# An attention stage's hand-written order, rewritten: new places for every step of a head, one batch in eight on TensorE, small operations on GpSimd

## The chip, the cores and the metric

One core of a Trainium2 chip runs the whole program. The metric is device time in microseconds (us) of one execution; lower is better. Five engines work side by side, each through its own queue in program order: TensorE (PE; its weight loads are listed as PEld), VectorE (DVE), ScalarE (ACT), GpSimd (POOL) and SyncE (SP), which here only issues DMA transfers. An engine stops at an instruction whose input or buffer isn't ready, and everything behind it in that queue waits too.

## The reference, cut to what matters

A two-layer decoder handles a prompt of 256 tokens and 8 sample sequences of 8 tokens together: a convolution layer, an MLP, an attention layer, an MLP. Only the attention layer is touched. It has 8 heads and three key groups per head, (window, dilation) = (128, 1), (512, 4), (2048, 16). For the samples each query sees its own tokens and cached keys at distances d, 2d, ..., window:

```python
idx = n_past + arange(S)[:, None] - dilation * arange(window // dilation + 1)[None, :]
s = einsum('bshe,bsnhe->bhsn', q, k_cat[:, idx]);  p = softmax(where(idx >= 0, s, -1e30))
o = einsum('bhsn,bsnhe->bshe', p, v_cat[:, idx])   # per group
# the three groups are merged by their softmax denominators, then  x += o @ w_o
```

Three groups merged this way are one softmax over all keys, and so the kernel computes it. At dilation 16 no two sample queries share a cached key, so there the product is elementwise: each query's vector times its own 128 keys, summed. That is done per batch (8 of them per head), once for keys and once for values.

## The kernel before, in words

Activations lie transposed, 128 channels by T = 320 tokens (256 prompt, 64 sample). Every fp32 product is three matmuls of fp32r halves: a weight is split by `split` (L117 to L127 of the kernel before) into `wh`, rounded by ScalarE (L126), and `wl`, the rest, subtracted by VectorE (L127), in halves of 1024 columns. Both have four buffers in a ring (`bufs=4`); raw weights have four of 1 MB, filled by SyncE.

In the attention stage nothing is scheduled automatically. Each step is added to a list with a position, and the list is sorted by position. Head h's weights (query, key and value for three groups: 9 chunks of 4 quarters) make 36 steps at positions 36h to 36h+35, 12 matmuls each; one position is thus one such step plus what is woven in. The rest of head h-1's attention (`side`) stands at 36h plus an offset, so it runs between the next head's 36 steps. After the last head the 32 steps of the output product `wo` take the place of the 36.

`Stream.run` walks the sorted list. Before a step that uses half number n of the weights it emits the splits up to half n+3 (`AHEAD = 3`); with four buffers the split of half n+3 has to wait until TensorE has finished with half n-1. A step's follow-up (`post`: the evacuation of its PSUM result by ScalarE or VectorE) is emitted after the next TensorE step. So one engine's queue holds splits and follow-ups mixed, and a split that waits for TensorE holds up what is behind it.

Steps of a head that matter below, with their offsets before:

- `qk` (3.2, 4.2, 5.2, 6.2 for dilation 4; 7.2 for dilation 1): sample scores of two groups, each step one half of split cached keys. Follow-up L811 to L813.
- `p_s(1)` (9.2): scores of the second 128 prompt rows, `o<-k,q` L746; its follow-up is a row maximum (L754, VectorE), exp (L618), reciprocal (L619), scaling (L620).
- `s_soft` (9.8): the same for the sample scores `S`: maximum over groups L822, then L618 to L620 on `S`.
- `p_t(1)` (13.6, 13.9): transposes of the second prompt softmax, `s<-cst,Sp` L762; `s_t`, `n_t` (14.6, 14.9): those of the sample softmax, L830 and L843.
- `pv` (18 to 26.8): sample output, L860, one half of split cached values each.
- `piece` (9 + 2.2b for keys, 26.6 + 2.2b for values, b = 0 to 7): dilation 16. SyncE fetches 512 KB into one of four buffers `al` (2.9 earlier); GpSimd copies a row `R` to all partitions (L643, the query or the probabilities) and multiplies in two halves (L645); VectorE sums (L650, 4.5 later). `row` writes `R` by small DMAs; `scores2` (6) transposes the query for it (L668).
- `q_fill` (1.2): `zz<-q` on ScalarE and a 128x64 subtraction on VectorE (L708); `new_s` (2.4): scores of the new tokens (L714), mask added by VectorE (L720); `v_t` (0, 0.3, 0.6): transposed values (L695, L696); `s_end`: adds the dilation-16 part to a head's sample output `os` (L887) and splits it.

Of the kernel before, what the change touches and what calls it, by code (L numbers as in the profile page):

```python
# [24 lines left out]
F32 = mybir.dt.float32  # L25
F32R = mybir.dt.float32r
# [12 lines left out]
G = 3  # L39
# [27 lines left out]
C_ID = 0  # L67
C_I2 = 128
C_SEL = 192
C_MN = 200  # L70
C_N = C_MN + NNEW
B_ID = 0
B_MS = 128
B_MP = B_MS + NPE
B_N = B_MP + 1152
CV_TAPS = {14: (11, 12), 15: (11, 12)}


# [1 line left out]
def decoder_step(ctx: ExitStack, tc: tile.TileContext, I, O):  # L80
# [119 lines left out]
    class Norm:  # L200
# [329 lines left out]
    with tc.tile_pool(name="attn", bufs=1) as ap:  # L530
# [8 lines left out]
        cb = ap.tile([128, B_N], BF, name="cb")  # L539
        pool.dma_start(cb, I["cb"])  # L540
        idb = cb[:, B_ID:B_ID + 128]

        B = {}

# [81 lines left out]
            todo.append((pos, len(todo), (pe_, post, chunk, part)))  # L626

        E2 = {}
        slots = [0]

        def piece(kind, h, b, at):


            n = slots[0]
            slots[0] += 1
            t = spread[:, n % 4]

            def fetch():
                sp.dma_start(t, I[kind + "2"][h, b])

            def mult():
                wide = spread[:, 4]
                pool.partition_broadcast(wide, E2[kind, h, b // 4][32 * (b % 4):32 * (b % 4) + 1, :])  # L643
                for c in (0, 512):
                    pool.tensor_mul(t[:, c:c + 512], t[:, c:c + 512], wide[:, c:c + 512])  # L645
# [7 lines left out]
            add(at - 2.9, None, fetch)  # L653
            add(at, None, mult)
            add(at + 4.5, None, total)

        def row(kind, h, half, src):

            r = E2[kind, h, half] = ap.tile([128, 1024], F32, name="R", bufs=2)
            for j in range(4):  # L660
                b = 4 * half + j
                sp.dma_start(r[32 * j:32 * j + 1, :], src[8 * b:8 * b + 8, :])

        def scores2(h, t0):

            def go():
                E2["qT", h] = ps = s_tile()
                pe.transpose(ps[:64, :128], B[h, 0, 2][:, SEQ:], ident)  # L668

            def post():  # L670
                q = ap.tile([64, 128], F32, name="qT")
                act.activation(q, E2["qT", h][:64, :128], AF.Copy)
                E2["q", h] = q
                row("k", h, 0, q)

            add(t0 + 6, go, post)
            add(t0 + 12, None, lambda: row("k", h, 1, E2["q", h]))
            for b in range(NB):
                piece("k", h, b, t0 + 9 + 2.2 * b)

        def side(h, t0):

# [21 lines left out]
            def q_fill():  # L704
                for g in range(2):
                    q = B[h, 0, g][:, SEQ:].rearrange("p (b s) -> p b s", b=NB)
                    act.activation(diag(g, 0), q, AF.Copy)
                    dve.tensor_sub(diag(g, 64), q, diag(g, 0))  # L708

            def new_s(pos):  # L710
                def go():
                    E["new"] = ps = s_tile()
                    for g in range(G):
                        pe.matmul(ps[:64, g * 64:g * 64 + 64], B[h, 0, g][:, SEQ:], B[h, 1, g][:, SEQ:], start=True,  # L714
                                  stop=True)

                def post():
                    E["S"] = S = ap.tile([64, NKEY + NNEW], F32, name="S")
                    E["m"] = small.tile([64, 8], F32, name="m")
                    dve.tensor_add(S[:, NKEY:], E["new"][:64, :NNEW], cst[:64, C_MN:C_MN + NNEW])  # L720
                    dve.tensor_reduce(E["m"][:, 0:1], S[:, NKEY:], axis=AX.X, op=OP.max)
                step(pos, go, post)

            def scores2_in(pos):
# [138 lines left out]

            def s_red():
                om = ap.tile([128, NB, 128], F32, name="Sp")
                E["orr"] = ap.tile([128, 128], F32, name="orr")
# [24 lines left out]
            for g in range(G):  # L891
                v_t(.3 * g, g)
            step(1.2, None, q_fill)
            new_s(2.4)
            scores2_in(2.7)
            p_s(3, 0)
            qk(0, 3.2, 4.2)
            qk(1, 5.2, 6.2)
            p_t(6.4, 0, 0)
            qk(2, 7.2)  # L900
            p_o(8.6, 0)
            p_s(9.2, 1)
            step(9.8, None, s_soft)
            p_t(13.6, 1, 0)
            p_t(13.9, 1, 3)
            s_t(14.6, 0, 5)
            n_t(14.9)
            p_o(17, 1)
            t2, dt = (13.5, 2.1) if last else (26.6, 2.2)
            step(11.5 if last else 22, None, lambda: row("v", h, 0, E["S"][:, NPE:NKEY]))  # L910
            step(11.5 if last else 30, None, lambda: row("v", h, 1, E["S"][:, NPE:NKEY]))
            for b in range(NB):
                piece("v", h, b, t0 + t2 + dt * b)
            for t in range(5):
                pv(18 + 2.2 * t, t)
            step(28.3, None, s_red)
            s_out(33.2)
            if not last:
                step(48.5, None, s_end)

        def qkv_steps(h):
            L = []
# [99 lines left out]
def _masks():  # L1022
    import numpy as np
    import ml_dtypes
    cst = np.zeros((128, C_N), np.float32)
    cst[:, C_ID:C_ID + 128] = np.eye(128)
    cst[:, C_I2:C_I2 + 64] = np.concatenate([np.eye(64), np.eye(64)])
    for p in range(128):
        cst[p, C_SEL + p % 64 // 8] = 1.0
    mn = np.full((64, G, 64), NEG, np.float32)  # L1030
    ms = np.full((128, NPE), NEG, np.float32)
    ms[64:] = 0
    mp = np.full((2, 128, G, 256), NEG, np.float32)
    for b in range(NB):
        for s in range(NS):
            p = 8 * b + s
            for g in range(G):
                for s2 in range(s + 1):
                    if (s - s2) % DILATIONS[g] == 0:
                        mn[p, g, 8 * b + s2] = 0  # L1040
            ms[p, [r for r in range(512) if r % 4 == s % 4 and r >= s]] = 0
            ms[p, [512 + r for r in range(128) if r >= s]] = 0
    for q in range(256):
        for g in range(G):
            for k in range(q + 1):
                if (q - k) % DILATIONS[g] == 0 and q - k <= WINDOWS[g]:
                    mp[q // 128, q % 128, g, k] = 0
    cst[:64, C_MN:] = mn.reshape(64, NNEW)
# [4 lines left out]
    cb[:, B_MP + 384:] = mp[1].reshape(128, 768)  # L1053
    return cst, cb.astype(ml_dtypes.bfloat16)


# [80 lines left out]
```

## Time and profile before

| | us |
|---|---|
| three runs | 3083.86, 3087.28, 3088.25 |
| median | 3087.28 |
| profiled execution, whole | 3087.17 |
| its span, first to last instruction | 3085.4 |
| TensorE busy in it | 2953.4 (96%) |
| VectorE, ScalarE, GpSimd busy | 1900.2, 1339.9, 895.9 |

The attention stage is the stretch in which GpSimd is busy a second time, from about 1365 to 2145 us. In the page's forty slices TensorE shows nine or more tenths everywhere except at the beginning and in slices 19 to 22 and 27, all in or just behind that stage. The page's chain of waits says what ended last; the view of waits says who waited for whom; timelines give the queue of one engine instruction by instruction.

### The profile page before, as it was taken

To read this page: it belongs to the slowest core of one execution; us is meant where nothing else is said; L and a number is where in the kernel's file an instruction comes from. 1 tells how busy PE (TensorE), PEld (TensorE's weight loads), DVE (VectorE), ACT (ScalarE), POOL (GpSimd) and SP (SyncE) were. 2 spreads that over 40 slices of the span, in tenths; PEclk is the share of its full clock that TensorE was granted. 3 is DMA by queue.
4 is the path that set the end of the run, shared out by engine and by line. 5 is a ranking of instruction groups with operands and counts; after the bars stand their busy time and mean duration, and the time that the engine had idled before them with its cause. 6 is when DMAs were issued, how large, how long until landed. Compare 5 with 4: busy or idle time off the path is not lost.

```text
span 3085.4 us, 47707 instructions
## 1 busy us (share of the span) xinstructions
PE 2953.4 (96%) x19600; PEld 2896.6 (94%) x19608; DVE 1900.2 (62%) x2258; ACT 1339.9 (43%) x1889; POOL 895.9 (29%) x597
## 2 busy tenths in 40 slices
PE   6999799999999999999999999988999999999998
PEld 6998799999999999999888888987999999999998
DVE  7989755444444444566898888888644444444444
ACT  7878544334334334434444444444433433433442
POOL 2767200000000000025999998996100000000000
PEclk9999899999999999999999999998999999999999
DMA  5443244444444444456767767765444444444442
GB/s 191 139 139 134 96 150 147 149 149 150 148 149 149 150 151 150 151 183 224 281 244 269 266 236 274 282 225 198 162 149 149 149 149 149 150 150 150 149 151 89
DMA packets 96522, 533.64 MB, mean 173 GB/s; under 512 B 13808, under 2 KB 21232, under 8 KB 43824
## 3 DMA queue, kind: packets, MB, share of 16 engines
q1 hardware_dynamic: 92624, 526.54, 48.3%
q10 hardware_dynamic: 3600, 3.57, 0.3%
q8 instruction: 153, 2.51, 0.3%
q14 instruction: 65, 0.53, 0.1%
q0 software_dynamic: 80, 0.49, 0.0%
HBM read 517.33 MB, written 12.70 MB: 172 GB/s over the span
## 4 chain that ended last, share of the span: by engine, by line
PE 74%; DVE 8%; POOL 7%; issue 4%; ACT 3%; DMA 3%; SPq 0%; DVEq 0%; POOLq 0%; ACTq 0%
PE mm L146 24%; PE mm L148 24%; PE mm L147 24%; POOL al L645 4%; DVE wl L127 4%; POOL al L643 2%; ACT wh L126 1%; DMA al<-v 1%; DMA R<-qT 1%; POOL pacc L378 1%; DVE tv L650 1%; PE o L860 0%; PE mm L368 0%; ACT prod L377 0%; DVE bl L157 0%
## 5 line engine op out<-in xcount | busy, mean ns | idle before, releaser
L127 DVE TENSOR_TENSOR wl<-raw,wh 128x1024 fp32r<-128x1024 f32 (+1 forms) x852 | 1159.1, 1366 | 727.4 <-ACT wh L126 721.8
L126 ACT ACTIVATE wh<-raw 128x1024 fp32r<-128x1024 f32 (+1 forms) x852 | 895.1, 1054 | 1457.4 <-PE mm L147 1272.1
L146 PE MATMUL mm<-bh,wh 128*128 128x320 f32 x3200 | 999.2, 312 | 12.5 <-ACT wh L126 12.0
L148 PE MATMUL mm<-bh,wl 128*128 128x320 f32 x3200 | 990.5, 310 | 1.0 <-DVE wl L127 0.4
L147 PE MATMUL mm<-bl,wh 128*128 128x320 f32 x3200 | 990.3, 309 | 0.0
L146 PE MATMUL mm<-ah,wh 128*128 128x320 f32 x2896 | 900.1, 311 | 34.7 <-ACT wh L126 12.5
L148 PE MATMUL mm<-ah,wl 128*128 128x320 f32 x2896 | 897.7, 311 | 3.4 <-DVE wl L127 3.3
L147 PE MATMUL mm<-al,wh 128*128 128x320 f32 x2768 | 855.4, 309 | 7.7 <-DVE al L154 4.0
L146 PEld LDWEIGHTS mm<-bh,wh 128*128 128x128 f32 x3200 | 605.2, 189 | 17.1 <-ACT wh L126 12.2
L147 PEld LDWEIGHTS mm<-bl,wh 128*128 128x128 f32 x3200 | 605.4, 189 | 3.1
L148 PEld LDWEIGHTS mm<-bh,wl 128*128 128x128 f32 x3200 | 604.7, 189 | 3.1 <-DVE wl L127 3.1
L146 PEld LDWEIGHTS mm<-ah,wh 128*128 128x128 f32 x2896 | 547.7, 189 | 40.8 <-ACT wh L126 14.3
L148 PEld LDWEIGHTS mm<-ah,wl 128*128 128x128 f32 x2896 | 547.5, 189 | 5.6 <-DVE wl L127 5.0
L147 PEld LDWEIGHTS mm<-al,wh 128*128 128x128 f32 x2768 | 520.9, 188 | 10.8 <-DVE al L157 5.3
L645 POOL TENSOR_TENSOR al<-al 128x512 f32<-128x512 f32 x256 | 449.6, 1776 | 32.2 <-DMA al<-k 11.8
L540 POOL DMA_DIRECT2D cb<-cb x1 | 0.7, 682 | 1011.7 <-PE mm L148 1011.7
L1017 POOL TENSOR_TENSOR bh<-bh,r 128x640 f32<-128x640 f32 x2 | 4.2, 2137 | 902.1 <-ACT r L1014 902.1
L643 POOL PARTITION_BROADCAST al<-R x128 | 218.2, 1705 | 87.1 <-DMA R<-qT 60.3
L378 POOL TENSOR_TENSOR pacc<-pacc,prod 128x320 f32<-128x320 f32 x168 | 180.9, 1112 | 76.2 <-ACT prod L377 75.2
L514 DVE TENSOR_TENSOR x<-x,mm 128x320 f32<-128x320 f32 x128 | 62.5, 488 | 178.6 <-PE mm L148 178.6
L509 DVE SCALAR_TENSOR_TENSOR sg<-mm,r 128x320 f32<-128x320 f32 x126 | 61.8, 492 | 162.2 <-PE mm L148 161.9
L388 DVE SCALAR_TENSOR_TENSOR s<-bl,wdw,s 128x320 f32<-128x320 f32 x272 | 130.0, 545 | 0.5 <-DMA out_cp<-gl 0.4
(205 smaller groups left out, 1718.7 us busy)
## 6 DMA issues: line engine op xcount, KB each, us to landing
raw<-w SPq DMA_DIRECT2D x252, 1024.0 KB
raw<-qkv SPq DMA_DIRECT2D x72, 1024.0 KB
raw<-pw SPq DMA_DIRECT2D x32, 1024.0 KB
al<-k SPq DMA_DIRECT2D x64, 512.0 KB
al<-v SPq DMA_DIRECT2D x64, 512.0 KB
raw<-k SPq DMA_DIRECT2D x16, 1024.0 KB
raw<-v SPq DMA_DIRECT2D x16, 1024.0 KB
raw<-pw2b SPq DMA_DIRECT2D x12, 1024.0 KB
```

The lines of the kernel that those rows point to most:

```text
L126: act.activation(wh[:, :n], r, AF.Copy)
L127: dve.tensor_sub(wl[:, :n], r, wh[:, :n])
L146: pe.matmul(ps, wh, xh, start=start, stop=False)
L147: pe.matmul(ps, wh, xl, start=False, stop=False)
L148: pe.matmul(ps, wl, xh, start=False, stop=stop)
L378: pool.tensor_add(pa, pa, pr_)
L388: dve.scalar_tensor_tensor(a, win(f, k), dw(f, k), a, op0=OP.mult, op1=OP.add)
L509: dve.scalar_tensor_tensor(t, ps, 0.0, norm.r, op0=OP.max, op1=OP.mult)
L514: dve.tensor_add(x[:, ob], x[:, ob], ps)
L643: pool.partition_broadcast(wide, E2[kind, h, b // 4][32 * (b % 4):32 * (b % 4) + 1, :])
L645: pool.tensor_mul(t[:, c:c + 512], t[:, c:c + 512], wide[:, c:c + 512])
L650: dve.tensor_reduce(E2["sum", kind, h][:, 8 * b:8 * b + 8], t.rearrange("p (a c) -> p a c", a=8), axis=AX.X, op=OP.add)
```

## The change

Every offset now comes from one table, `POS`. Apart from new numbers, five edits:

1. Batch 5 of each eight (`BY_PE`) is no longer spread by GpSimd. The row `R` is written as a high and a low half in two partitions; TensorE multiplies two rows of ones with them (K = 2, 512 columns, twice) into PSUM, and VectorE multiplies the fetched piece with that. For this the query (`ql`) and the probabilities (`pl`, step `weights`) are split too.
2. The small subtractions and the addition with two SBUF inputs, in `q_fill` and `s_end`, move from VectorE to GpSimd. The copy of `os` moves from VectorE to ScalarE.
3. The new tokens' mask is added by a matmul in PSUM, not by VectorE; ScalarE copies the result.
4. A fetch waits in the order for the sum that frees its buffer.
5. Sample transposes now come ahead of the second prompt transposes.

```diff
+BY_PE = (5,)
+POS = dict(qT=6.03, k1=12.64, k=9.27, kd=2.2, lag=4.5, ahead=3.6, lagp=1.5, ... qf=1.52,
+           new=3.63, s2=3.93, ps0=1.52, a0=4.43, a1=6.22, a2=6.76, a3=7.39, pt0=4.57, b0=10.58, po0=13.84, ps1=14.07,
+           soft=12.08, st=16.88, nt=15.12, pt1=16.99, pt2=17.66, po1=21.07, v0=22.79, v1=31.21, v=26.67, vd=2.2,
+           pv=19.88, pvd=1.62, red=28.38, out=34.53, end=48.77, lv0=12.69, lv1=13.5, lv=14.5, lvd=2.44)
...
+            def on_pe(c):
+                def go():
+                    box["ps"] = ps = s_tile()
+                    pe.matmul(ps, onesr[j:j + 2], E2[kind, h, b // 4].bitcast(F32R)[j:j + 2, 512 * c:512 * c + 512],
+                              start=True, stop=True)
+                def post():
+                    dve.tensor_mul(t[:, 512 * c:512 * c + 512], t[:, 512 * c:512 * c + 512], box["ps"])
+                add(at + .3 * c, go, post)
...
+            add(max(at - POS["ahead"], ends[n - 4] + .01 if n > 3 else 0), None, fetch)
...
-                    dve.tensor_sub(diag(g, 64), q, diag(g, 0))
+                    pool.tensor_sub(diag(g, 64), q, diag(g, 0))
...
+                    pe.matmul(ps[:64, :NNEW], idb[:, :64], cb[:, B_MN:B_MN + NNEW], start=True, stop=False)
...
-                    dve.tensor_add(S[:, NKEY:], E["new"][:64, :NNEW], cst[:64, C_MN:C_MN + NNEW])
+                    act.activation(S[:, NKEY:], E["new"][:64, :NNEW], AF.Copy)
...
-                    dve.tensor_copy(E["os"], E["so"][:, :64])
+                    act.activation(E["os"], E["so"][:, :64], AF.Copy)
...
-                dve.tensor_add(E["os"], E["os"], E2["sum", "v", h])
-                split_in(oh[:, h, SEQ:], ol[:, h, SEQ:], E["os"])
+                pool.tensor_add(E["os"], E["os"], E2["sum", "v", h])
+                act.activation(oh[:, h, SEQ:], E["os"], AF.Copy)
+                pool.tensor_sub(ol[:, h, SEQ:], E["os"], oh[:, h, SEQ:])
```

Line numbers in the changed kernel are higher: the splits L126 and L127 become L133 and L134, the softmax lines L618 to L620 become L626 to L628. Three places in the order, all in the middle of a head, show what moved.

ScalarE before, from the query transpose's copy (`qT`) to the second prompt softmax (`Sp<-o,mx`):

```order
L672 ACTIVATE qT<-s 64x128
L811 ACTIVATE S<-s 64x512
L765 ACTIVATE Sp<-s 128x384
L126 ACTIVATE wh<-raw 128x1024 x2
L811 ACTIVATE S<-s 64x128
L153 ACTIVATE ah<-s 128x128
L618 ACTIVATE S,l<-S,mn 64x960
L620 ACTIVATE S<-S,l 64x960
L126 ACTIVATE wh<-raw 128x1024
L618 ACTIVATE Sp,l<-o,mx 128x768
L620 ACTIVATE Sp<-Sp,l 128x768
```

And ScalarE in the changed kernel, from the last splits of that stretch to the same softmax:

```order
L133 ACTIVATE wh<-raw 128x1024 x3
L853 ACTIVATE S<-s 64x512
L133 ACTIVATE wh<-raw 128x1024 x2
L853 ACTIVATE S<-s 64x128
L133 ACTIVATE wh<-raw 128x1024
L626 ACTIVATE S,l<-S,mn 64x960
L628 ACTIVATE S<-S,l 64x960
L930 ACTIVATE ah<-os 128x64
L133 ACTIVATE wh<-raw 128x1024
L160 ACTIVATE ah<-s 128x128
L626 ACTIVATE Sp,l<-o,mx 128x768
```

Three splits more now stand between the first sample scores and the sample softmax, and between the two softmaxes stands the copy of the finished head's output (`ah<-os`), which before came behind both.

VectorE before, from the last sample scores (`S<-s,S` of 128 columns) to the reciprocal of the second prompt softmax:

```order
L812 TENSOR_TENSOR S<-s,S 64x128
L813 TENSOR_REDUCE m<-S 64x1
L650 TENSOR_REDUCE tv<-al 128x8
L154 TENSOR_TENSOR ah<-s,ah 128x128
L822 TENSOR_REDUCE mn<-m 64x1
L619 RECIPROCAL l<-l 64x1
L127 TENSOR_TENSOR wl<-raw,wh 128x1024
L754 TENSOR_REDUCE mx<-o 128x1
L619 RECIPROCAL l<-l 128x1
```

And VectorE in the changed kernel, over the same stretch:

```order
L134 TENSOR_TENSOR wl<-raw,wh 128x1024 x2
L854 TENSOR_TENSOR S<-s,S 64x128
L855 TENSOR_REDUCE m<-S 64x1
L134 TENSOR_TENSOR wl<-raw,wh 128x1024
L996 TENSOR_TENSOR v_18202<-mm,r 128x320
L864 TENSOR_REDUCE mn<-m 64x1
L627 RECIPROCAL l<-l 64x1
L672 TENSOR_REDUCE tk<-al 128x8
L134 TENSOR_TENSOR wl<-raw,wh 128x1024
L161 TENSOR_TENSOR ah<-s,ah 128x128
L796 TENSOR_REDUCE mx<-o 128x1
```

A split and an evacuation (`v`) came in ahead of the sample maximum `mn`; between `mn` and the prompt maximum `mx` there is still one split `wl`, and the sum `tk` and the split of `ah` moved in beside it.

GpSimd in the changed kernel, where the addition for the finished head stands:

```order
L653 ISA al<-R 128x1024
L655 TENSOR_TENSOR al<-al 128x512 x2
L653 ISA al<-R 128x1024
L655 TENSOR_TENSOR al<-al 128x512 x2
L929 TENSOR_TENSOR os<-os,tv 128x64
L931 TENSOR_TENSOR ah<-os,ah 128x64
```

The two pieces in front are the first two key pieces of the next head; before, GpSimd had only pieces.

## Rows read from the trace of the kernel before

**Rows 1.** Busy time by stretch: engine sums, granted clock, DMA share, GB/s.

```profile
1366.00:1371.00 5.00, 5.00 (x25) 5.00 (x25) 2.33 (x3) 1.33 (x2) 1.69 (x1) 0.66 0.03 7
1881.20:1973.60 92.40, 85.76 (x560) 81.61 (x560) 80.19 (x77) 38.96 (x57) 83.37 (x48) 0.98 0.71 262
1912.40:1916.80 4.40, 0.00 (x0) 0.00 (x0) 3.34 (x4) 1.92 (x4) 4.22 (x4) 1.00 0.11 41
1916.90:1920.30 3.40, 3.40 (x14) 3.40 (x15) 2.60 (x4) 0.85 (x1) 3.22 (x3) 0.50 0.01 2
```

**Rows 2.** TensorE's waits from 1300 to 2150 us: total, times, longest.

```profile
PE s L762 <- ACT Sp L620: 29.0, 7, 4.6
PE s L799 <- DVE S L720: 9.1, 7, 1.7
...
PE s L714 <- DVE q L942: 3.5, 4, 1.9
PE s L695 <- DVE os L881: 2.9, 3, 1.7
```

**Rows 3.** TensorE's timeline at the query transposes of heads 0, 6 and 7.

```profile
1365.91 0.27 PE L668 MATMUL s<-cst,q 128*64 128x128 f32 x1 [2.21 <-issue]
...
1893.82 0.27 PE L668 MATMUL s<-cst,q 128*64 128x128 f32 x1
...
1986.78 0.27 PE L668 MATMUL s<-cst,q 128*64 128x128 f32 x1
```

**Rows 4.** VectorE's timeline, 1907 to 1914 us, among head 6's steps.

```profile
1907.79 0.14 DVE L822 TENSOR_REDUCE mn<-m 64x1 f32<-64x4 f32 x1
...
1911.46 2.28 DVE L127 TENSOR_TENSOR wl<-raw,wh 128x1024 fp32r<-128x1024 f32 x1 [2.12 <-ACT wh L126]
1913.67 0.94 DVE L754 TENSOR_REDUCE mx<-o 128x1 f32<-128x768 f32 x1
```

**Rows 5.** TensorE's timeline in the same period, 1890 to 1923 us.

```profile
1890.74 0.40 PE L803 MATMUL s<-wh,zz 128*128 128x512 f32 x1
...
1891.67 0.31 PE L146 MATMUL mm<-bh,wh 128*128 128x320 f32 x1
...
1897.36 0.23 PE L799 MATMUL s<-cb 128*128 128x128 bf16 x1
...
1899.22 0.36 PE L146 MATMUL mm<-bh,wh 128*128 128x320 f32 x1
...
1910.22 0.31 PE L148 MATMUL mm<-bh,wl 128*128 128x320 f32 x1
...
1911.98 0.31 PE L148 MATMUL mm<-bh,wl 128*128 128x320 f32 x1
1916.86 1.54 PE L762 MATMUL s<-cst,Sp 128*128 128x128 f32 x6 [4.56 <-ACT Sp L620]
...
1921.00 0.52 PE L830 MATMUL s<-cst,S 64*128 64x64 f32 x5
...
1922.04 0.41 PE L146 MATMUL mm<-bh,wh 128*128 128x320 f32 x1
```

**Rows 6.** Instruction groups by shape, 1511 to 1973 us: count, busy, mean ns.

```profile
L645 POOL TENSOR_TENSOR al<-al 128x512 f32<-128x512 f32 x161 | 289.0, 1815 | 24.5 <-DVE wl L127 8.9 <-DMA al<-k 8.4 <-DMA al<-v 0.8
L127 DVE TENSOR_TENSOR wl<-raw,wh 128x1024 fp32r<-128x1024 f32 x140 | 241.0, 1742 | 26.0 <-ACT wh L126 24.4 <-PE s L762 1.6
L126 ACT ACTIVATE wh<-raw 128x1024 fp32r<-128x1024 f32 x140 | 146.4, 1056 | 152.9 <-PE mm L147 95.2 <-PE o L860 36.0 <-PE s L803 15.4
...
L944 DVE TENSOR_TENSOR v<-mm,r 128x320 f32<-128x320 f32 x15 | 7.2, 483 | 0.2
...
L708 DVE TENSOR_TENSOR zz<-q,zz 128x64 fp32r<-128x64 f32 x10 | 10.8, 1115 | 0.0
```

**Rows 7.** SyncE's issue of a head's query rows, and GpSimd's first piece with them.

```profile
1901.41 2.69 SPq L662 DMA_DIRECT2D R<-qT  x4
...
1908.76 1.29 POOL L643 PARTITION_BROADCAST al<-R  x1 [1.81 <-DMA R<-qT]
```

More of the change, by code (lines that the diff above doesn't have):

```diff
@@ L69 @@
 C_SEL = 192
-C_MN = 200
-C_N = C_MN + NNEW
+C_N = 200
 B_ID = 0
@@ L541, in decoder_step @@
         idb = cb[:, B_ID:B_ID + 128]
+        onesr = ones.bitcast(F32R)
         B = {}
@@ L642, in mult @@
                 wide = spread[:, 4]
-                pool.partition_broadcast(wide, E2[kind, h, b // 4][32 * (b % 4):32 * (b % 4) + 1, :])
-                for c in (0, 512):
-                    pool.tensor_mul(t[:, c:c + 512], t[:, c:c + 512], wide[:, c:c + 512])
+                pool.partition_broadcast(wide, E2[kind, h, b // 4][j:j + 1, :])
+                for c in range(0, 1024, HALF):
+                    pool.tensor_mul(t[:, c:c + HALF], t[:, c:c + HALF], wide[:, c:c + HALF])
+            def on_pe(c):
+                box = {}
+                def go():
[5 more added lines that the diff above has]
+                add(at + .3 * c, go, post)
             def total():
@@ L651, in total, with pieces, row @@
                                   axis=AX.X, op=OP.add)
[L653 to L657, printed above, removed]
+            add(max(at - POS["ahead"], ends[n - 4] + .01 if n > 3 else 0), None, fetch)
+            if b in BY_PE:
+                on_pe(0)
+                on_pe(1)
+            else:
+                add(at, None, mult)
+            add(ends[n], None, total)
+        def pieces(kind, h, t0, dt):
+            i = 0
+            for b in range(NB):
+                piece(kind, h, b, t0 + dt * (i - .5 if b in BY_PE else i))
+                i += b not in BY_PE
+        def row(kind, h, half, src, hi, lo):
             r = E2[kind, h, half] = ap.tile([128, 1024], F32, name="R", bufs=2)
@@ L671, in post @@
                 q = ap.tile([64, 128], F32, name="qT")
[L672 to L679, printed above, removed]
+                qh = ap.tile([128, 128], F32R, name="orr")
+                ql = ap.tile([64, 128], F32R, name="ql")
+                ps = E2["qT", h][:64, :128]
+                act.activation(q, ps, AF.Copy)
+                if BY_PE:
+                    split_in(qh[:64], ql, ps)
+                E2["q", h] = q, qh[:64], ql
+                row("k", h, 0, *E2["q", h])
+            add(t0 + POS["qT"], go, post)
+            add(t0 + POS["k1"], None, lambda: row("k", h, 1, *E2["q", h]))
+            pieces("k", h, t0 + POS["k"], POS["kd"])
         def side(h, t0):
@@ L712, in go @@
                     E["new"] = ps = s_tile()
+                    pe.matmul(ps[:64, :NNEW], idb[:, :64], cb[:, B_MN:B_MN + NNEW], start=True, stop=False)
                     for g in range(G):
[L714 to L715 removed]
+                        pe.matmul(ps[:64, g * 64:g * 64 + 64], B[h, 0, g][:, SEQ:], B[h, 1, g][:, SEQ:], start=False,
+                                  stop=(g == G - 1))
                 def post():
@@ L894, in side @@
[L894 to L910, printed above, removed]
@@ L911, in side, with weights @@
-            step(11.5 if last else 30, None, lambda: row("v", h, 1, E["S"][:, NPE:NKEY]))
-            for b in range(NB):
-                piece("v", h, b, t0 + t2 + dt * b)
+            def weights():
+                p = E["S"][:, NPE:NKEY]
+                ph = ap.tile([64, 128], F32R, name="qT")
+                pl = ap.tile([64, 128], F32R, name="ql")
+                if BY_PE:
+                    split_in(ph, pl, p)
+                E2["p", h] = p, ph, pl
+                row("v", h, 0, *E2["p", h])
@@ new lines, in side @@
+            P = POS
+            for g in range(G):
+                v_t(P[f"vt{g}"], g)
+            step(P["qf"], None, q_fill)
+            new_s(P["new"])
+            scores2_in(P["s2"])
+            p_s(P["ps0"], 0)
+            qk(0, P["a0"], P["a1"])
+            qk(1, P["a2"], P["a3"])
+            p_t(P["pt0"], 0, 0)
+            qk(2, P["b0"])
+            p_o(P["po0"], 0)
+            p_s(P["ps1"], 1)
+            step(P["soft"], None, s_soft)
+            s_t(P["st"], 0, 5)
+            n_t(P["nt"])
@@ L914, in side @@
+            p_t(P["pt1"], 1, 0)
+            p_t(P["pt2"], 1, 3)
+            p_o(P["po1"], 1)
+            z = "l" if last else ""
+            step(P[z + "v0"], None, weights)
+            step(P[z + "v1"], None, lambda: row("v", h, 1, *E2["p", h]))
+            pieces("v", h, t0 + P[z + "v"], P[z + "vd"])
             for t in range(5):
-                pv(18 + 2.2 * t, t)
-            step(28.3, None, s_red)
-            s_out(33.2)
+                pv(P["pv"] + P["pvd"] * t, t)
+            step(P["red"], None, s_red)
@@ L918, in side @@
+            s_out(P["out"])
             if not last:
-                step(48.5, None, s_end)
+                step(P["end"], None, s_end)
         def qkv_steps(h):
```

28 lines of the change are left out of this document (17 added, 11 removed).

## The prediction

> **What bounds the kernel now.** I read busy time by stretch first. In a head's period TensorE works 85.8 of 92.4 us, GpSimd 83.4, VectorE 80.2 [rows 1]: three engines near their limit, so the question is which of them is waited for. The view of TensorE's waits answers it: one wait carries most, the transposes of the second prompt softmax (L762), 29.0 us in 7 waits, 4.1 each; three smaller ones, for the mask addition (L720), for the query (L942) and for the copy of `os` (L881), make 15.5, or 2.2 per period [rows 2]. The timelines show where the 4.1 comes from: the sample maximum `mn` starts at 1907.79, behind it VectorE waits for ScalarE, the split takes until 1913.67, only then comes the prompt maximum, and TensorE goes on at 1916.86 [rows 4, 5]: 9.07 us from `mn` to TensorE. The stall costs a second time: in the 3.4 us behind it the granted clock is 0.50, the 1.2 GHz level, after 4.4 us without a matmul [rows 1], which loses 1.7. So a period wastes 4.1 + 1.7 + 2.2 = 8.0 us; the rest, about 84.5, is TensorE's work. A full period is 92.96 from head 6's query transposes to head 7's [rows 3]. The seven stalls lie in the periods of heads 2 to 7 and behind the last head.
>
> **The change part by part, per period.**
>
> The three small waits: the mask leaves VectorE for a matmul, the copy of `os` for ScalarE, and the step that waited for the query moves from offset 2.4 to 3.63. All are then ready in time: −2.2. The first prompt scores, which need the same query, move forward to 1.52. I count nothing for them: from the query's last matmul to there TensorE has two steps and more, over 3.5 us, in which VectorE has a split (1.74 [rows 6]) and the query's evacuation to do first; where that cover fails, it costs the longest such wait of before, 1.9 [rows 2].
>
> Work added on TensorE: four matmuls of 512 columns. The row nearest is a `qk` step, four such matmuls from 1890.74 to 1891.67, 0.93 [rows 5]. With two rows of weights instead of 128 they may be cheaper, down to nothing; at double price they cost 1.9. I take 0.93, with 0.1 for the mask: +1.0.
>
> A new wait at step 8. The rings have four buffers, and splits are emitted three halves ahead, so the half of step 8 takes the buffer of the half that steps 6 and 7 use. Before, it took that of the key step at 5.2, with two qkv steps and two key steps in between. Now the last dilation-4 key steps stand at 6.76 and 7.39, and only the one at 7.39 lies between step 7 and step 8. From the end of step 7 the half needs ScalarE's 1.06 and VectorE's split, mean 1.74 [rows 6]; TensorE has 0.93 of work and two matmuls (0.3) before it needs the low half. 1.06 + 1.74 − 1.23 = 1.6; with a split as short as ScalarE's 1.06 it is 0.9, with the longest shown, 2.28 [rows 4], 2.1. GpSimd is then between two heads' pieces and waiting for `R` [rows 7], so I take the lower middle, +1.4. Behind it on ScalarE's queue stand the next splits and the copy of the query, from which SyncE writes `R`: what is late there reaches GpSimd (rival B).
>
> The second prompt softmax. I count from the start of step 8. Twelve matmuls take 1.76 (1910.22 to 1911.98), the dilation-1 step 1.86 (1897.36 to 1899.22) [rows 5]. TensorE needs 12.9 from step 8 to L762 in the trace (1899.22 to 1911.98, and 0.15 for the last matmul); now three more steps (5.3), the dilation-1 step and the sample transposes (1921.00 to 1922.04, 1.04) come before it: ready at 21.1. The other side: the split of the half two behind step 11 gets its buffer at the end of step 11, at 4 × 1.76 + 1.86 = 8.9. ScalarE 1.06 with hand-over 0.2: 10.2; VectorE a split w, the two small steps of the sample scores (0.5), another split w, an evacuation 0.48 [rows 6]: `mn` at 11.2 + 2w. From there 9.07 as before, but with w in place of its split of 2.21 (1911.46 to 1913.67), and 0.5 for the copy of the finished head and a split of `ah` that now stand between: 7.4 + w. Sum 18.6 + 3w: 23.8 with the mean split, 21.8 and 25.4 with 1.06 and 2.28. The stall shrinks from 4.1 to 2.7, bounds 0.7 and 4.3; GpSimd's waits shorten some splits, so 2.4. The clock: at 1365.91 a stall of 2.21 [rows 3] is followed by 0.66 on average over 5 us [rows 1], a fall too. So 1.7 stays lost behind this stall; behind the stall of 1.4 I count no fall, with 1.7 as its upper end.
>
> The Trainium skill (SBUF — State Buffer, Who interferes with whom) has a VectorE instruction contend with GpSimd when both its inputs are in SBUF, and not when one is in PSUM. The splits (two in SBUF, 2.28 at worst) and the evacuations (0.483 mean for 320 columns) agree with it. By that rule every split beside an idle GpSimd would be near its short end and the total near the first rival's; by the mean row it is the sum here.
>
> VectorE's balance: off go two subtractions of 1.1 (L708), two operations of `s_end`, the mask and a copy, none longer than L708; on come four multiplications from PSUM, at L944's rate 0.483 × 512/320 = 0.77 each, and two splits of a row [rows 6]. Within a microsecond of nothing. GpSimd loses two pieces of 1.3 + 2 × 1.8 = 4.9 [rows 6, 7] and gets four operations of 64 columns, which the trace does not show on it: between 0.2 and one 512-column multiplication, 1.8, each; I take L708's 1.1. 83.4 − 9.8 + 4.4 = 78.
>
> The Trainium skill (GPSIMD Engine Reference, Engine selection) puts two-input elementwise work on VectorE, GpSimd being about twice as slow. No run here shows GpSimd at 64 columns. By the page an estimate of 4 × 2.2 = 8.8 would bring GpSimd back to 82, which costs nothing in this sum and feeds the second rival.
>
> Per period: −8.0 + 1.0 + 1.4 + 2.4 + 1.7 = −1.5, times six = −9. Head 1's period had no stall at L762: there +1.0 + 1.4, perhaps half of 2.4, less the small waits: +1. The last head: its value pieces on GpSimd decide when the output product can end; seven instead of eight is −4.9, the smaller stall −1.7, and the small waits −2.2: −9. SyncE's queue gets two row DMAs more, 2.69/4 = 0.7 each [rows 7], and fetches that stand in order behind the sum that frees their buffer; weight loads behind them start up to 1.3 later, which four raw buffers hide, and at worst it adds its 1.3. Sum −17 from the profiled execution's 3087.17 (span 3085.4 and 1.8 around it; the median is 3087.28): **3070**.
>
> **The rivals.**
>
> A, the stall goes altogether. Splits run at the short end and the softmax arrives within some tenths: then no clock falls, −8.0 + 1.0 + 0.9 = −6.1, times six = −37, last head −11: 3040. For it: GpSimd has 14 pieces instead of 16; 18.6 + 3w at 1.06 leaves only 0.7. Against it: the new order places two splits and an evacuation ahead of `mn`, and the mean split is 1.74 [rows 6].
>
> B, slower: ScalarE waits for GpSimd. The copy of the finished head (`ah<-os`) now stands on ScalarE's queue between the two softmaxes, behind GpSimd's addition, which stands behind two key pieces. ScalarE gets there 17.4 after step 8 begins (`mn` at 14.7 and 2.7 for exp and scaling). GpSimd needs the row `R`, two pieces (9.8) and the addition (1.1): it must begin by 6.5. In the trace it begins at 1908.76 [rows 7], 9.5 after step 8 (1899.22 [rows 5]), 7.3 after SyncE's issue at 1901.41. For B: that row, taken over, is 2.9 too late. Against: the issue depended on a weight load ahead of it on SyncE's queue, and the new order asks for fewer loads there. It decides from about 9 on (17 us over seven stalls, 2.4 each, eat the gain). One piece late, 4.9: −1.5 + 4.9 = +3.4, times six, with head 1 and −4 at the end: +17, 3104.
>
> C, VectorE is the bound. The five value steps stand in 6.5 positions instead of 8.8: 6.5 × 1.76 + 5 × 0.93 = 16.1 of TensorE's work, in which VectorE has eight or nine splits, 14 to 16 us at the mean, and sums and the new multiplications beside them. Three halves in hand may not cover this; one split not ready costs 1.06 + 1.74 = 2.8 per period, six times +17: 3087, no change.
>
> **How the numbers follow.** The forecast has 0.42, A 0.20, B 0.20, C 0.18. What counts as no change is within 0.2%, 3081 to 3093. The forecast's own bounds (stall 0.7 to 4.3, step 8 at 0.9 to 2.1, a fall of the clock fewer or more) give it 3050 to 3086, of which 0.04 lies within no change. A is faster; C divides into 0.04 faster, 0.10 same, 0.04 slower; B into 0.02 and 0.18. Faster 0.62, same 0.16, slower 0.22. The range reaches to A's and B's values, 3036 to 3102.
>
> **What would show it.** In the profile after: L804 (the old L762) with 2 to 3 us of wait per period on ScalarE's scaling; at the qkv step behind the last dilation-4 key step a wait of 1 to 2 us for `wh` or `wl`; no wait on the mask or the copy of `os`; GpSimd near 78 us per period; half clock once per period. B would show as ScalarE waiting at `ah<-os` for GpSimd, C as TensorE waiting for `wl` between the value steps. A period under 87 us or over 94 would prove the forecast wrong.

## The result, and the profile after

| | before | after |
|---|---|---|
| median of 4 runs, us | 3087.04 (3083.86 to 3088.25) | 3041.05 (3040.30 to 3042.71) |
| span of the profiled execution | 3085.4 | 3038.8 |
| query transposes of heads 1, 2 and 7 start at | 1436.5, 1524.3, 1986.8 | 1434.0, 1520.4, 1951.2 |
| mean period of heads 2 to 6 | 92.5 | 86.2 |
| span behind head 7's query transposes | 1098.6 | 1087.6 |
| GpSimd, VectorE busy, whole span | 895.9, 1900.2 | 811.6, 1867.1 |

The ratio is 0.9853, with a 95% interval from 0.9836 to 0.9870: 46 us less where I forecast 17. Of the 46.6 us between the two spans, 2.5 are gained up to head 1, 1.5 in head 1's period (87.9 to 86.4), 31.6 in the five periods of heads 2 to 6 (6.3 each), and 11.0 behind, where one more period's gain and the last head lie.

TensorE's waits come first, from 1300 to 2150 us (engine, line, what it waits for: total us, times, longest). They answer to [rows 2].

```profile
PE mm L155 <- DVE wl L134: 5.0, 3, 2.9
PE s L786 <- ACT vn L742: 4.4, 7, 0.6
PE s L804 <- ACT Sp L628: 2.8, 6, 1.6
PE s L705 <- issue: 2.2, 1, 2.2
```

The second prompt transposes, L762 before and L804 now, waited 29.0 us and wait 2.8. The three smaller waits of [rows 2] are gone. New is the first prompt scores' wait for the copy of v (L786), 0.6 per head. The longest waits for `wl` lie behind the last head.

The windows of the changed kernel (busy us of PE, PEld, DVE, ACT, POOL with counts; then granted clock, DMA share, GB/s) answer to [rows 1]: behind head 0's query transposes, two whole periods, and the stretch behind head 6's second prompt transposes.

```profile
1365.60:1371.00 5.40, 5.40 (x38) 5.40 (x39) 3.36 (x4) 1.49 (x3) 2.63 (x2) 1.00 0.15 24
1779.00:1865.20 86.20, 85.41 (x567) 80.77 (x566) 76.37 (x77) 40.45 (x61) 74.05 (x47) 1.00 0.77 282
1865.20:1951.20 86.00, 85.37 (x568) 80.78 (x566) 76.44 (x77) 40.46 (x61) 73.75 (x48) 1.00 0.77 284
1890.90:1894.30 3.40, 3.40 (x27) 3.33 (x26) 2.87 (x4) 2.88 (x6) 3.31 (x3) 1.00 0.83 282
```

TensorE is busy in 85.4 of 86.0 us: the period has become its own work. The clock stays at 1.00, the 2.4 GHz level; 27 matmuls stand where before, at 0.50, there were 14. GpSimd fell from 83.4 to 74.

The chain that the forecast was built on, in head 6, whose step 8 starts TensorE at 1869.89. VectorE's timeline (start, us, engine, line, operation, tiles, idle time and releaser) answers to [rows 4]:

```profile
1878.21 1.22 DVE L134 TENSOR_TENSOR wl<-raw,wh 128x1024 fp32r<-128x1024 f32 x1 [1.04 <-ACT wh L133]
1879.36 0.29 DVE L854 TENSOR_TENSOR S<-s,S 64x128 f32<-64x128 f32 x1
1879.68 0.28 DVE L855 TENSOR_REDUCE m<-S 64x1 f32<-64x128 f32 x1
1879.99 1.54 DVE L134 TENSOR_TENSOR wl<-raw,wh 128x1024 fp32r<-128x1024 f32 x1
1881.56 0.49 DVE L996 TENSOR_TENSOR v<-mm,r 128x320 f32<-128x320 f32 x1
1881.97 0.14 DVE L864 TENSOR_REDUCE mn<-m 64x1 f32<-64x4 f32 x1
...
1885.78 1.75 DVE L134 TENSOR_TENSOR wl<-raw,wh 128x1024 fp32r<-128x1024 f32 x1 [1.11 <-ACT wh L133]
...
1887.65 0.94 DVE L796 TENSOR_REDUCE mx<-o 128x1 f32<-128x768 f32 x1
```

ScalarE in the same head:

```profile
1866.22 1.06 ACT L133 ACTIVATE wh<-raw 128x1024 fp32r<-128x1024 f32 x1 [1.65 <-PE s L845]
...
1877.12 1.06 ACT L133 ACTIVATE wh<-raw 128x1024 fp32r<-128x1024 f32 x1 [2.59 <-PE s L845]
...
1878.90 1.06 ACT L133 ACTIVATE wh<-raw 128x1024 fp32r<-128x1024 f32 x1 [0.56 <-PE mm L154]
...
1884.56 0.24 ACT L930 ACTIVATE ah<-os 128x64 fp32r<-128x64 f32 x1
...
1889.85 0.94 ACT L628 ACTIVATE Sp<-Sp,l 128x768 f32<-128x768 f32 x1 [0.23 <-DVE l L627]
```

And TensorE at the transposes, with no wait in front, which answers to the stall of 4.56 in [rows 5]:

```profile
1890.97 0.55 PE L804 MATMUL s<-cst,Sp 128*128 128x128 f32 x3
```

`mn` comes 12.1 us after step 8 begins, the scaling ends at 20.9, and TensorE gets there at 21.1, the figure that the forecast had for TensorE. In the six other heads the scaling ends at 21.0 to 21.5, and TensorE waits 0.4 at most: the stall is gone, with nothing to spare. ScalarE passes `ah<-os` (L930) without a wait.

### The profile page after: what moved, and what is told of

Its sections match the earlier page's. It is cut to its first block, busy times and chain, and to the rows that moved or that the text cites. A ratio compares the mean times of both kernels' runs of the same rounds, so it can differ in the third digit from the quotient of the medians.

```text
span 3038.8 us, 47790 instructions
## 1 busy us (share of the span) xinstructions
PE 2947.5 (97%) x19648; PEld 2885.9 (95%) x19648; DVE 1867.1 (61%) x2258; ACT 1346.2 (44%) x1921; POOL 811.6 (27%) x581
## 4 chain that ended last, share of the span: by engine, by line
PE 87%; DVE 5%; ACT 3%; DMA 2%; issue 2%; POOL 1%; SPq 0%; DVEq 0%; ACTq 0%; POOLq 0%
PE mm L153 27%; PE mm L155 27%; PE mm L154 27%; DVE wl L134 2%; PE o L902 1%; ACT wh L133 1%; DMA al<-k 1%; POOL pacc L385 1%; PE s L845 1%; PE s L846 1%; PE mm L375 0%; DMA al<-v 0%; PE s L817 0%; ACT prod L384 0%; DVE bl L164 0%
## 5 line engine op out<-in xcount | busy, mean ns | idle before, releaser
L134 DVE TENSOR_TENSOR wl<-raw,wh 128x1024 fp32r<-128x1024 f32 x852 | 1136.8, 1337 | 715.2 <-ACT wh L133 714.4
L133 ACT ACTIVATE wh<-raw 128x1024 fp32r<-128x1024 f32 x852 | 896.1, 1055 | 1465.4 <-PE mm L154 1296.9
L155 PE MATMUL mm<-bh,wl 128*128 128x320 f32 x3200 | 986.1, 308 | 1.4 <-DVE wl L134 1.4
L155 PE MATMUL mm<-ah,wl 128*128 128x320 f32 x2896 | 895.7, 310 | 4.1 <-DVE wl L134 3.9
L155 PEld LDWEIGHTS mm<-bh,wl 128*128 128x128 f32 x3200 | 601.2, 188 | 2.1 <-DVE wl L134 2.1
L155 PEld LDWEIGHTS mm<-ah,wl 128*128 128x128 f32 x2896 | 546.2, 189 | 6.1 <-DVE wl L134 5.4
L655 POOL TENSOR_TENSOR al<-al 128x512 f32<-128x512 f32 x224 | 384.7, 1738 | 45.3 <-DMA al<-v 19.2
L653 POOL PARTITION_BROADCAST al<-R x112 | 188.8, 1685 | 76.6 <-DMA R<-qT 56.4
```

The lines of the kernel that those rows point to most:

```text
L133: act.activation(wh[:, :n], r, AF.Copy)
L134: dve.tensor_sub(wl[:, :n], r, wh[:, :n])
L155: pe.matmul(ps, wl, xh, start=False, stop=stop)
L653: pool.partition_broadcast(wide, E2[kind, h, b // 4][j:j + 1, :])
L655: pool.tensor_mul(t[:, c:c + HALF], t[:, c:c + HALF], wide[:, c:c + HALF])
```

## The experiments

All line numbers of e1 to e4 are one lower than those of the changed kernel. A difference within some 6 us (0.2%) counts as no change.

### Places and unloading, crossed: e1, e2, e3

The code allows both halves of the change to be taken back apart. e1: the old offsets and `BY_PE = ()`; e2: the old offsets alone; e3: `BY_PE = ()` alone. All three keep the mask by a matmul, the copy of `os` on ScalarE, the small operations on GpSimd, and a fetch's place behind the sum that frees its buffer.

```diff
-BY_PE = (5,)
+BY_PE = ()                       # e1, e3
-POS = dict(qT=6.03, k1=12.64, ... ps1=14.07, soft=12.08, st=16.88, nt=15.12, pt1=16.99, ...)
+POS = dict(qT=6, k1=12, ... ps1=9.2, soft=9.8, st=14.6, nt=14.9, pt1=13.6, ...)   # e1, e2
```

> Old places of all steps, all eight batches spread by GpSimd, but the other edits kept (mask by a matmul, copy of os by ScalarE, small operations on GpSimd). Theory 'places' (the gain of 46 us comes from where the steps stand, which lets the second prompt softmax be done before TensorE asks for it, and so keeps the clock): 3080 to 3090, TensorE still waits some 4 us per head at the second prompt transposes and half clock follows once per head. Rival 'unloading' (fewer GpSimd pieces shorten VectorE's splits and with them the softmax): 3080 to 3090 as well. Rival 'small edits' (the mask, the copy and the small operations make the gain): below 3055.

> Old places of all steps, but batch 5 of each dilation-16 spread by TensorE, and the other edits. 'Places': 3075 to 3090, the stall at the second prompt transposes stays at 3 to 4 us per head and the clock still falls behind it. Rival 'unloading': 3041 to 3055, the stall is gone although the steps stand where they stood.

> New places, all eight batches spread by GpSimd (no matmul of two rows, no multiplication on VectorE). 'Places': 3035 to 3050, as fast as the changed kernel or faster by the added TensorE work of some 0.9 per head, no fall of the clock in the attention stage; only behind the last head are some 5 us more. Rival 'unloading': 3070 or more, with the stall back at the second prompt transposes. A third reading, that the new places need the unloading because ScalarE's copy of the finished head waits for GpSimd: 3060 to 3100, with TensorE's stall behind that copy.

| median us (ratio to before, interval) | 8 batches on GpSimd | 7 on GpSimd, 1 by TensorE |
|---|---|---|
| old places | e1 3098.20 (1.0041, 1.0029 to 1.0054) | e2 3094.42 (1.0025, 1.0016 to 1.0035) |
| new places | e3 3072.20 (0.9955, 0.9943 to 0.9968) | after 3041.05 (0.9853) |

The kernel before, run beside each group of experiments, stood at 3085.7 to 3087.3. Neither half gives the gain alone: against the kernel before, the unloading alone gains nothing and the new places alone 15. In the old places the unloading gives 3.8, no change by the bound, in the new ones 31.2; the new places give 26.0 with eight batches and 53.4 with seven. And in the old places the edits without both make the kernel 11 slower than before. TensorE's waits in e1, 1300 to 2160 us, show a reason:

```profile
PE s L844 <- POOL zz L748: 21.8, 7, 3.3
PE s L803 <- ACT Sp L627: 12.5, 7, 3.5
PE s L755 <- DVE q L993: 10.9, 6, 3.3
```

The small subtraction for `zz`, now on GpSimd's queue behind its pieces, is late for the first key step (L844), 3.1 per head. An operation of 0.3 us on a nearly full engine costs its place in the queue, not its length. In e2 GpSimd has room, and that wait shrinks to 2.0 in all; what stays are the softmax and the splits:

```profile
PE s L803 <- ACT Sp L627: 18.8, 7, 3.7
PE mm L154 <- DVE wl L133: 8.1, 10, 1.7
PE s L840 <- DVE m L762: 7.9, 6, 1.6
```

e2 also pays for four matmuls per head, 11.5 by e9 below; if they cost the same there, the 3.8 is what is left behind that price. The unloading in the old places with the small operations left on VectorE was not run.

e3 is the instructive one. Its period is 90.2, and one period by the windows view reads

```profile
1879.90:1970.10 90.20, 85.25 (x563) 81.56 (x562) 76.14 (x71) 39.99 (x59) 86.48 (x53) 0.98 0.74 267
```

GpSimd is busy 86.5 of 90.2, and over the four periods from 1609 to 1970 its waits sum to less than 5 us: it has work queued nearly all the time, and most of the rest is the time between its 53 instructions. GpSimd is the bound. Only head 1's period, which GpSimd enters with nothing left over (it waits 20.8 us for its first row there), runs at 84.2. GpSimd's timeline in head 6 and ScalarE's next to it:

```profile
1899.92 1.30 POOL L652 PARTITION_BROADCAST al<-R  x1
1901.31 2.53 POOL L654 TENSOR_TENSOR al<-al 128x512 f32<-128x512 f32 x2
1903.79 0.32 POOL L928 TENSOR_TENSOR os<-os,tv 128x64 f32<-128x64 f32 x1
```

```profile
1904.14 0.26 ACT L929 ACTIVATE ah<-os 128x64 fp32r<-128x64 f32 x1 [2.34 <-POOL os L928]
```

ScalarE stands at `ah<-os` for GpSimd's addition: rival B of the prediction, in a kernel with one batch more on GpSimd. TensorE waits 4.3 to 4.8 at the transposes in six of seven times (29.3 in all), and the clock falls behind or within six of six such stalls from 1550 to 2001.

### Is it that one copy? e8

```diff
-... end=48.77 ...
+... end=57.5 ...     # with BY_PE = (), as e3
```

> New places with all eight batches on GpSimd (the kernel of e3_new_gps, 3072), but the end of the finished head (GpSimd's addition, ScalarE's copy that waits for it, GpSimd's subtraction) moved from 48.77 to 57.5, behind the second prompt softmax. Theory 'ScalarE waits for GpSimd' (that copy alone holds the softmax back by 2.3 to 6): no stall at the prompt transposes, period 84.5 to 86, 3035 to 3050. Rival 'late sums' (GpSimd's last value pieces end late, and VectorE's sums of them stand ahead of the sample maximum, which comes 14.5 after the first quarter instead of 12.1): the stall falls by less than half, 3058 to 3072.

Measured: 3068.01 (ratio 0.9944, 0.9927 to 0.9960), 4 less than e3, no change by the bound. The stall at the transposes shrank from 4.7 to 2.6, and the time came back at other places (L788 waits 1.0 per head for the query, L155 5.3 in all for splits). What is left of the stall comes from VectorE, in part as the second reading had it: `mn` comes 14.6 after step 8 begins, where the changed kernel has it at 12.1 to 12.5. In head 6 VectorE works without a gap up to it, with one sum of the finished head more than in the changed kernel. First the rows of e8 (step 8 begins at 1883.47):

```profile
1882.81 4.54 DVE L134 TENSOR_TENSOR wl<-raw,wh 128x1024 fp32r<-128x1024 f32 x2
...
1890.82 1.20 DVE L672 TENSOR_REDUCE tv<-al 128x8 f32<-128x1024 f32 x1
...
1893.08 1.21 DVE L672 TENSOR_REDUCE tv<-al 128x8 f32<-128x1024 f32 x1
...
1898.08 0.14 DVE L864 TENSOR_REDUCE mn<-m 64x1 f32<-64x4 f32 x1
```

And the same two splits in the changed kernel, with GpSimd's row, which shows it idle beside them:

```profile
1869.03 2.34 DVE L134 TENSOR_TENSOR wl<-raw,wh 128x1024 fp32r<-128x1024 f32 x2
```

```profile
1873.43 1.30 POOL L653 PARTITION_BROADCAST al<-R  x1 [5.62 <-DMA R<-qT]
```

On average a split took 2.27 here beside the full GpSimd and 1.17 there beside the idle one. The period of e8 is 90.2 still, GpSimd is busy 86.9 of it, and over the five periods from 1518 to 1969 us it waits only 1.8 us:

```profile
1788.70:1878.80 90.10, 84.84 (x563) 80.09 (x563) 76.93 (x71) 39.54 (x59) 86.85 (x53) 1.00 0.73 267
```

```profile
POOL ah L931 <- ACT ah L930: 1.8, 5, 0.4
```

The copy was a symptom: without that wait the time is lost elsewhere. That an earlier `mn` would gain nothing either is argued from the same 90.2 and was not run. In both orders tried, the order chooses where TensorE waits for a full GpSimd, not whether. The unloading takes this bound away: with seven batches GpSimd has 74 us of work, and TensorE's 86 decide.

### What the way over TensorE costs: e9

```diff
             if b in BY_PE:
-                on_pe(0)
-                on_pe(1)
+                pass
```

> The changed kernel with the four matmuls of two rows and the four multiplications of a head left out: batch 5 is not weighted, so this part of the result is missing; GpSimd still does seven batches. It measures what TensorE's way of spreading costs where TensorE is the bound. By the forecast's term (0.93 per head for four matmuls of 512 columns): 3033 to 3036. By the trace of the changed kernel (two of them in 0.66 us): 1.3 per head, 3030 to 3033. If the multiplications on VectorE also hold TensorE: below 3028. If TensorE isn't the bound: 3039 to 3042.

Measured: 3029.59 (ratio 0.9816, 0.9803 to 0.9829), 11.5 less than the changed kernel, 1.4 per head; the mean period of heads 2 to 6 falls from 86.2 to 84.9. Four matmuls of two rows, 0.33 us from one start to the next, make 1.3 of it, as the changed kernel's TensorE timeline has it (two of them, then the value step):

```profile
1897.07 0.73 PE L662 MATMUL s<-R,ones 2*128 2x512 f32 x2
1897.73 0.50 PE L902 MATMUL o<-wh,zz 128*128 128x512 f32 x1
```

I had put them at 0.93 for four. The price is a net one: in e9 the wait at the second prompt transposes is back (7.8 in seven times), and the wait for the copy of v is gone from the list. No cost of the four multiplications on VectorE shows beside that.

### Where the small operations run: e4

```diff
-                    pool.tensor_sub(diag(g, 64), q, diag(g, 0))
+                    dve.tensor_sub(diag(g, 64), q, diag(g, 0))
-                pool.tensor_add(E["os"], E["os"], E2["sum", "v", h])
+                dve.tensor_add(E["os"], E["os"], E2["sum", "v", h])
...
```

> The changed kernel with the four small two-input operations of a head (two of q_fill, two of s_end) back on VectorE. If they cost VectorE 1.1 each by the row of before and stand on the path to the softmax: +1 to +3 per head, 3048 to 3065. If VectorE has room for them: 3040 to 3045, no change.

Measured: 3040.28 (0.9850, 0.9837 to 0.9864), no change. In its profiled execution the periods of heads 2 to 6 are 0.6 longer (86.8), and the stretch behind head 7's query transposes is 3.1 shorter, so that the two cancel. The words "small operations on GpSimd" name no part of the gain in this order.

### Distance alone, and a stall put back: e5, e6

```diff
-pt1=13.6, pt2=13.9     # e5: old places, BY_PE = (5,)
+pt1=15.2, pt2=15.5
```

```diff
-pt1=16.99, pt2=17.66   # e6: the changed kernel
+pt1=15.2, pt2=15.5
```

> Old places with batch 5 on TensorE (the kernel of e2_old_pe, 3094), but the two prompt transposes moved from 13.6 and 13.9 to 15.2 and 15.5, two qkv steps later, behind the sample's transposes. Theory 'distance' (what the new places give is time between the softmax and the matmuls that want it): TensorE's wait there, 2.7 per head, goes, and the clock falls behind it with it, 2.7 + 1.7 to 3.4 for seven heads: 3050 to 3065; the rest to 3041 is the waits for the mask's evacuation and for splits. Rival 'softmax itself is late' (what stands ahead of it on ScalarE and VectorE is the point, and is as late as before): the wait shrinks by less than half, 3075 to 3095.

> The changed kernel with the two prompt transposes moved from 16.99 and 17.66 to 15.2 and 15.5, one qkv step and the sample's transposes earlier, some 2.5 us of TensorE's work. It puts a stall of about that length back, and asks what a stall costs with the clock. If the clock falls behind each: 2.5 + 1.7 per head, 3065 to 3080. If it does not: 2.5 per head, 3055 to 3062. If nothing is lost since the waits behind are taken over: 3041 to 3048.

e5: 3093.36 (1.0025, 1.0016 to 1.0034) against e2's 3094.42, nothing gained. The wait for the softmax is gone from the list, and others took its place; TensorE's waits, 1300 to 2160 us:

```profile
PE mm L155 <- DVE wl L134: 10.1, 8, 1.7
PE s L804 <- ACT pn L889: 6.8, 4, 3.3
PE s L841 <- DVE m L763: 6.7, 5, 1.9
PE s L845 <- POOL zz L749: 5.9, 3, 2.0
```

The first theory missed; the second's time came, but not for its reason, since the wait that was to stay went. Moving one wanted step away from its producer is not enough where splits and tiles of PSUM, the memory that TensorE writes to, bind next (`pn` is the evacuation that frees such a tile). How many of the other steps had to move with it was not tried.

e6: 3066.84 (0.9939, 0.9924 to 0.9954), 25.8 slower than the changed kernel, from two numbers. The stall is back at 2.2 to 2.5 per head. Two periods and the stretches behind their stalls, by the windows view:

```profile
1436.00:1526.00 90.00, 86.82 (x568) 82.07 (x567) 72.96 (x75) 40.53 (x60) 67.30 (x43) 0.98 0.72 261
1704.50:1792.90 88.40, 85.34 (x566) 80.79 (x566) 73.99 (x77) 40.67 (x61) 71.35 (x47) 1.00 0.74 273
1463.00:1466.40 3.40, 3.40 (x17) 2.95 (x15) 2.10 (x1) 1.26 (x2) 3.22 (x3) 0.50 0.54 169
1730.30:1733.70 3.40, 3.40 (x26) 3.14 (x27) 1.84 (x2) 2.25 (x5) 3.22 (x4) 1.00 0.90 304
```

Here are the stalls with the clock's answer beside them:

```profile
1461.86 0.87 PE L804 MATMUL s<-cst,Sp 128*128 128x128 f32 x6 [2.49 <-ACT Sp L628]
...
1730.26 0.88 PE L804 MATMUL s<-cst,Sp 128*128 128x128 f32 x6 [2.36 <-ACT Sp L628]
```

After 2.49 the clock fell to the 1.2 GHz level, after 2.36 it did not, and of this kernel's seven stalls there up to 2000 us three were followed by a fall (2.49, 2.33, 2.20) and four were not (2.46, 2.36, 2.48, 2.34). Periods with a fall take 90.0, those without 88.4 to 88.7: a fall costs 1.5, near the 1.7 of the prediction. Of the 24.6 between the two spans, 16.9 lie between heads 1 and 7, 1.9 before (a fall behind head 0) and the rest behind. The time lies in the range that I had for a fall behind each stall, though only three of seven had one. And a stall of the size that I had forecast gives nearly the time that I had forecast (3070).

### Toward a faster version: e7, e10, e11, e12

```diff
-vt2=1.76, ps0=1.52, pt0=4.57
+vt2=1.76, ps0=2.3,  pt0=4.57    # e7
+vt2=2.2,  ps0=3.2,  pt0=5.5     # e10, e12
```

```diff
+        def by_pe(kind, h):      # e11, e12; asked in the place of BY_PE for each piece
+            return (2, 5) if kind == "v" and h == H - 1 else BY_PE
```

> The changed kernel with the first prompt scores moved from 1.52 to 2.3, behind the third transposes of v instead of between the second and the third, which takes away the wait of 0.6 per head for the copy of v. If that wait is a loss of its own: 4 less, 3036 to 3038. If the time is only waited elsewhere: 3040 to 3043.

> The changed kernel with the three transposes of v and the first prompt scores in four different gaps between qkv steps (vt2 from 1.76 to 2.2, ps0 from 1.52 to 3.2, pt0 from 4.57 to 5.5). e7_ps0_later moved the wait for the copy of v and did not remove it, since two of the four still stood in one gap. If the wait then goes: 0.87 per head for seven heads, 3034 to 3038. If a new wait for PSUM or the mask's evacuation takes its place: 3040 to 3050.

> The changed kernel with batch 2, beside batch 5, of the last head's values on TensorE, so that GpSimd has six pieces there instead of seven. Theory 'the last head's end waits for GpSimd' (its last piece ends at 2090, the output product waits at 2094 and behind): up to 5 less, 3035 to 3038. Rival 'TensorE's waits there come from the splits and the evacuations': 3040 to 3043.

> The edits of e10_vt_apart and e11_last_head together, as a version that may beat the changed kernel: 3028 to 3036 if both gains come, 3036 to 3041 if one does.

| | median us | ratio to before, interval |
|---|---|---|
| e7 | 3042.07 | 0.9857, 0.9842 to 0.9872 |
| e10 | 3039.66 | 0.9846, 0.9833 to 0.9860 |
| e11 | 3045.37 | 0.9866, 0.9852 to 0.9879 |
| e12 | 3041.88 | 0.9854, 0.9840 to 0.9867 |

None differs from the changed kernel by more than the bound, though all four runs of e11 (3043.42 to 3045.99) lie above all of the changed kernel's. e7 only handed the wait to the transposes of v (L736, 4.4 in seven times). e10 does remove it, and the mean period of heads 2 to 6 goes from 86.2 to 85.8; but in its profiled execution the clock fell once at 1366.5, behind head 0, where in that of the changed kernel it did not, so that it began head 1's period 2.4 later (1436.4 against 1434.0) and head 7's at the same time (1951.1). If it is a gain, it is below what these runs resolve. In e11 GpSimd has one piece fewer behind the last head, and yet waits there (total us, times, longest, 2050 to 2105):

```profile
POOL os L932 <- DVE tv L675: 5.8, 1, 5.8
POOL al L658 <- DVE wl L134: 4.9, 1, 4.9
```

The piece that it lost came back as a wait for VectorE's queue; the last head is not bound by the number of pieces alone.

## Why the prediction was wrong

The direction was right, and the time fell into the range, but the forecast of 3070 failed, and the measured 3041 lies beside the first rival's 3040, to which I had given 0.20. By the prediction's steps, per period:

- **The three small waits, −2.2: right.** None of them is in the list of waits after. But "I count nothing" for the first prompt scores missed a wait of 0.6 for the copy of v; the cover that I named was for the query, and the wait is for v.
- **Work added on TensorE, +1.0: too small.** 1.3 by the rows, 1.4 by e9.
- **A new wait at step 8, +1.4: wrong.** There is none. The premise was that buffers go round strictly in turn, so that step 8's half had to wait for the end of step 7. The row at 1866.22 shows its `wh` released by a key step (L845), before step 7 had begun. Its buffer was that of a half of cached keys, which was through earlier.
- **The remaining stall before the second prompt transposes, +2.4: wrong; none in head 6, 2.8 us over the whole stage.** This is the step that decides. TensorE's side, ready at 21.1, came out exactly. The other side, 18.6 + 3w = 23.8, was 20.9. Of the 2.9 too much, 2.6 lie ahead of `mn` (12.1 where I had 14.7). I put two splits and the two small steps of the sample scores behind the release at the end of step 11. The rows show that the first split (`wh` at 1877.12, `wl` at 1878.21) is released by the dilation-1 key step, 1.7 before step 11 ends, and that it and the small steps (0.29, 0.28) run while ScalarE rounds the next half. Only one split stands behind: one w of 1.74 and the 0.5 were counted on the path that lay beside it. (Of ScalarE's splits, too, only one was added between the first sample scores and the sample softmax: three where two stood, not three more.) The rest is w itself, 1.54 there, not 1.74. From `mn` to the end of the scaling it takes 8.8; I had 7.4 + w = 9.1.
- **The fall of the clock stays, +1.7: wrong, and it hung on the step before.** With that stall gone no fall is left: none from 1300 to 2091 us. Even the premise was too firm. The stall of 2.21 at 1365.91 before [rows 3] was followed by a fall, one of 2.18 at 1365.60 after was not, and e6 shows both at the same length.
- **GpSimd 78: too high, 74.** The four small operations cost 0.31 to 0.34 each on it up to 2000 us (L749, L929, L931), not L708's 1.1, which is 3.1 of the difference. L708's 1.1 was VectorE's time beside a working GpSimd: the two such subtractions that found GpSimd idle took 0.22 and 0.23 (at 1422 before). So the estimate of 2.2 each doubled a disturbed time. The Trainium skill (GPSIMD Engine Reference, Engine selection) makes two-input work on GpSimd about twice as slow; the undisturbed rows agree in direction, 0.33 against 0.22. Beside GpSimd's multiplications VectorE took up to 1.32 in e4, and there the measurement is the other way round.
- **GpSimd as cover, not as a bound: incomplete.** I asked only which engine is waited for now. By e3 and e8 sixteen pieces and the small operations make a period of 90.2, in both orders tried. Without the unloading the gain was e3's 15. The prediction credits the unloaded batch with a shorter GpSimd time and finds no use for it but in the last head; it is worth 31 us in the new places.

The windows view closes the sum over the five periods of heads 2 to 6. TensorE's idle time in them fell from 32.0 us to 3.7, or by 5.7 per period: the stall and the three small waits went, the wait for the copy of v came. Its busy time fell from 430.4 to 427.1, or by 0.7: the clock gave back some 1.9 per period (four falls of 3.4 us, and one with 5.1 us of work at 0.50 from 1546.6 on), and the four matmuls took 1.3. Together that is the measured −6.3. Behind head 7, taking one such period of 6.3 off the 11.0, the last head gave about 4.7 where I had 9; e11 says that one piece less is not one piece's time.

**The rivals.** A was right in its result, and half in its reason. Its −6.1 per period is near the measured −6.3 by luck in one place: its 0.9 at step 8 isn't there, and 0.6 at the first prompt scores and 0.3 more of matmuls stand for it. The splits did shorten, 1.60 on average from 1500 to 1960 us where [rows 6] had 1.74, with 1.71 in e3, where GpSimd has all its pieces; the Trainium skill (SBUF — State Buffer, Who interferes with whom) agrees with that direction. But the splits in the stall's way were not at 1.06; one of them was not in the way. B didn't happen, by a margin that the rows give: GpSimd's addition ended at 1884.21, ScalarE was there at 1884.56. e3 shows that the wait is real with one batch more on GpSimd; e8 shows that taking it away alone does not give the time back. (The range was to reach B's 3104, and its end of 3102 does not.) C, `wl` late between the value steps, is not in the list of waits; the waits for `wl` stand behind the last head.

**Order or unloading?** Shown by the crossing: neither alone. The order gives TensorE its time back as long as GpSimd keeps up, and the unloaded batch lets it keep up. An order made for eight pieces was not run.

## What to carry to other kernels

When a change takes a wait off the busiest engine, work out at once what the next engine's own time per period is, gaps between its instructions included, since the new order cannot go below it; two parts of a change may each be worth little and much together. Before a chain is added up, place each of its terms before or after the event that releases the chain, by the queue's rows: a whole split that runs ahead of the release costs nothing. Don't assume which buffer a ring will hand out where halves are used in another order than they are loaded; the releaser in the trace tells.

## What was not expected of the hardware

- A subtraction of 128x64 takes 0.33 us on GpSimd. On VectorE it took 0.22 beside an idle GpSimd and up to 1.33 beside a working one.
- A matmul with two rows of weights and 512 columns is no cheaper than one with 128: 0.33 us, against 0.23 for those of a key step.
- Stalls of TensorE of the same length, 2.2 to 2.5 us, were followed by the 1.2 GHz level in some heads and not in others, in one execution of one kernel (e6).
- GpSimd's broadcast of a row of 1024 takes 1.30 us or 2.14 to 2.37, both in one head of e3, where the engine hardly waits.
